# Folding a layer's normed activations over tokens ahead of the Fourier projection

## The chip, the cores and the metric

The kernel runs on one core of a Trainium2 chip. What is measured is the device time in microseconds (us) of one execution; lower is better. TensorE (PE) multiplies matrices, VectorE (DVE), ScalarE (ACT) and GpSimd (POOL) do everything else, and SyncE (SP) issues the transfers between the chip's memory and the on-chip buffer. PE writes into eight PSUM banks.

## The reference

Two layers over 1040 tokens (16 meta tokens and 1024 others) of 1024 features. In each layer the normed input goes through one projection whose columns belong to four groups (pooling, Fourier, a bidirectional state-space scan "SSD", attention); each group mixes in its own way, is gated, and one output projection adds the result to the input.

```python
for i in range(DEPTH):
    hn = rmsnorm(h, norm_w[i])
    proj = jnp.einsum("bld,de->ble", hn, w_in[i])
    (u_pool, g_pool, u_fft, g_fft, xbc, z, dt_raw, q, k, v, g_attn) = jnp.split(proj, points, axis=-1)
    y_pool = multiscale_pool(u_pool, pool_w[i], pool_scale[i]) * jax.nn.silu(g_pool)
    y_fft = fourier_mix(u_fft, fourier_w[i]) * jax.nn.silu(g_fft)
    y_ssd = ssd_mixer(xbc, z, dt_raw, ...)
    y_att = gqa_axial(q, k, v, q_norm_w[i], k_norm_w[i], cos, sin) * jax.nn.silu(g_attn)
    mixed = jnp.concatenate([y_pool, y_fft, y_ssd, y_att], axis=-1)
    h = h + jnp.einsum("ble,ed->bld", mixed, w_out[i])

def fourier_mix(u, w):
    mixed = jnp.fft.fft2(u.astype(jnp.float32), axes=(1, 2), norm="ortho").real
    return jnp.einsum("blc,cd->bld", mixed.astype(u.dtype), w)
```

The Fourier group has 512 columns, u_fft. The real part of its two-dimensional transform needs u at token n and at token 1040 - n only as their sum (for cosines) and their difference (for sines), and columns c and 512 - c likewise.

## The kernel before

Activations lie with the features on the 128 partitions and the tokens along the row: the input h is eight tiles d = 0 to 7 of 128 x 1040. Tokens go in three chunks (`CH`) of 348, 346 and 346. A 32-bit product is made of three matmuls: every operand is split into a high half, a cast on ACT (line 128), and a low half, a subtraction on DVE (line 129), and `mm3` issues high x high (line 132), high x low (133) and low x high (134) into one PSUM bank. `prenorm` writes the normed input as such halves, `s.hh` and `s.hl` (lines 186 to 188; the subtractions are shared between DVE and POOL by a table).

A projection of one 128-column tile (`proj`) is three chunks x eight d x three matmuls. Its raw weights come in two transfers of 256 KB (`wraw`, the tiles named `wr`, four buffers), and `wsplit` makes their halves `wh` and `wl` of 128 x 512 (lines 128, 129).

The Fourier projection `fft_proj` handles two column tiles i, each once as the sum of columns c and 512 - c (`kind` 0) and once as their difference (`kind` 1). The sum or difference is taken of the raw weights (line 278), so each (i, kind) is one ordinary projection of 1040 columns. Behind it DVE folds the projected u over tokens (line 283, 519 columns) and once more over half of that (`fold2`, line 289), and the result goes to memory (`md`), from where the Fourier stages read it after attention.

The order of work: each generator yields after a few instructions, `weave` runs several generators in shares, and a scheduler then fixes the order of the instructions on every engine. A layer starts with `prenorm` of the three chunks, woven with the key and value projections `kv` (`att_kv`), each chunk of keys followed by its norm and rotary work on ACT and DVE (lines 142 to 145 and 549 to 600; its last rows, line 578 before and 600 after, take the low halves of the keys, 64 x 346). The five attention stages are each woven with a share of a "fill", a long list of projections that depend on nothing but `s.hh` and `s.hl`. The string `FO` gives the fill's order: U, P, F, Z and D are projections (U is the pooling group's input, D the SSD's time steps), each C is a convolution of the SSD, R is `fft_proj`. `FN` gives the units of fill in each attention stage, `FK` the units woven with the last chunk of keys and values, and one unit is four steps. `s.h` is dropped when the prenorm is done and its eight tiles of the pool `big` (30 tiles) are used again.

The names psmm, pssc, pspv, psxx, psy are PSUM banks; smq and smn are short rotary and norm tiles.

Of the kernel before, what the change touches and what calls it, by code (L numbers as in the profile page):

```python
# [52 lines left out]
def hybrid_trunk(ctx: ExitStack, tc: tile.TileContext, io, out, depth=DEPTH):  # L53
# [22 lines left out]
    PB, KB, NPF, NACC = 2, 3, 14, 4  # L76
# [31 lines left out]
    def chunk_tile(tag, dt=F32):  # L108
        return phase["p"].tile([128, 348], dt, name=nm(tag), tag=tag, bufs=NPF if tag == "pf" else PB)
# [53 lines left out]
    def prenorm(l, s, ci):  # L163
        if ci == 0:
            s.hh = [big(F32R) for _ in range(8)]
            s.hl = [big(F32R) for _ in range(8)]
        c0, cw = CH[ci]
        ss = ps("xx")
        n = PN[l][ci]
        for i in range(n):  # L170
            eng = (nc.gpsimd, nc.vector)[i % 2]
            for d in range(i, 8, n):
                sq = sm()
                nc.scalar.activation(sq[:, :cw], s.h[d][:, c0:c0 + cw], AF.Square)
                if d == i:
                    acc = sq
                else:
                    eng.tensor_tensor(acc[:, :cw], acc[:, :cw], sq[:, :cw], op=ALU.add)
            nc.tensor.matmul(ss[:, :cw], ones, acc[:, :cw], start=(i == 0), stop=(i == n - 1))
        yield  # L180
        rs = rstd(ss[:, :cw], cw, D)
        yield
        for d in range(8):
            t = sm()
# [1 line left out]
            nc.vector.scalar_tensor_tensor(t[:, :cw], s.h[d][:, c0:c0 + cw], vec(l, V_NW + d), rs[:, :cw], op0=ALU.mult, op1=ALU.mult)
            nc.scalar.copy(hi, t[:, :cw])
            (nc.gpsimd if d in PG[ci] else nc.vector).tensor_tensor(lo, t[:, :cw], f(hi), op=ALU.subtract)  # L188
            if d % 2:
                yield  # L190
# [56 lines left out]
    def spill_dt(l, s):  # L247

        s.gd["dt"] = drp.tile([1, 40, L], F32, name=nm("gd"))
# [6 lines left out]
        for c0, cw in CH:  # L256
# [7 lines left out]
            nc.scalar.copy(t[0:40, :cw], p[64:104, :cw])  # L264
            nc.vector.tensor_tensor(t[0:40, :cw], t[0:40, :cw], p[0:40, :cw], op=ALU.add)
            nc.sync.dma_start(s.gd["dt"][0, :, c0:c0 + cw], t[:40, :cw])

    def fft_proj(l, s):

        for i in range(2):  # L270
            c = 1 - i
            for kind in range(2):
                ws = []
                for k in (0, 4):
                    a = wraw(io["w1"][l, T_FA + i, :, k:k + 4])
                    b = wraw(io["w1"][l, T_FB + i, :, k:k + 4])
                    r = (a, b)[kind]
                    nc.vector.tensor_tensor(r[:, :, c:], a[:, :, c:], b[:, :, c:], op=(ALU.add, ALU.subtract)[kind])
                    ws += wsplit([r])
                u = yield from proj_copy(s, ws)  # L280

                def fold(o, u, op):
                    nc.vector.tensor_tensor(o[:, 1:HALF], u[:, 1:HALF], u[:, HALF + 1:L][:, ::-1], op=op)

                def fold2(dst, v):

                    w = big()[0:v.shape[0], 0:HALF + 1]
                    for o, n0, n1, op in ((0, 0, 32, ALU.add), (32, 0, 4, ALU.subtract), (36, 32, 260, ALU.add), (265, 4, 260, ALU.subtract)):
                        nc.vector.tensor_tensor(w[:, o:o + n1 - n0], v[:, n0:n1], v[:, HALF + 1 - n1:HALF + 1 - n0][:, ::-1], op=op)
                    nc.scalar.copy(w[:, 264:265], v[:, HALF // 2:HALF // 2 + 1])  # L290
                    nc.sync.dma_start(dst, w)
                if i == 0 and kind == 1:

                    y = big()[0:1, 0:HALF + 1]
                    nc.vector.tensor_copy(y, u[0:1, 0:HALF + 1])
                    fold(y, u[0:1], ALU.add)
                    fold2(s.md["ny"], y)
                if kind == 1:
                    nc.vector.memset(u[:, 0:HALF + 1:HALF], 0.0)
                fold(u, u, (ALU.add, ALU.subtract)[kind])  # L300
                fold2(s.md["r"][2 * i + kind], u[:, 0:HALF + 1])
                yield

# [415 lines left out]
    def ssd_dt(l, s):  # L719
# [9 lines left out]
        for q0 in range(0, NQ, 2):  # L729
# [289 lines left out]
    for l in range(depth):  # L1019
# [184 lines left out]
```

## Time and profile before

| | before |
|---|---|
| median of 3 runs | 2110.99 us (2107.0 to 2111.65) |
| profiled execution | 2113.91 us |
| its span, first to last instruction | 2112.0 us |
| mean granted clock of TensorE | 0.981 |
| PE busy | 1991.0 us (94%), 11880 matmuls |
| DVE busy | 1397.0 us (66%) |
| ACT busy | 1012.7 us (48%) |
| POOL busy | 369.0 us (17%) |

A line "L129" is line 129 of the kernel. A row of the trace's groups gives the line, the engine, the operation, what it writes and reads with sizes, the count, the busy time, the mean of one in ns, and the idle time of the engine just before, with what ended it. A row of a timeline starts with the start in us and the duration. Matmuls overlap in such rows, so their pace is read from their starts. A window's row gives the stretch, its length and the busy time of each engine in it.

### The profile page before, as it was taken

What the parts mean: (1) busy time and instruction counts of PE and PEld (TensorE: products, weight loads), DVE (VectorE), ACT (ScalarE), POOL (GpSimd) and SP (SyncE); (2) the same over time, 40 slices, a digit from 0 to 9 for tenths busy, and PEclk for the clock granted to TensorE, in tenths of its full rate; (3) what the DMA queues carried; (4) which work ended last, traced back from release to release, by engine and by line L of the source; (5) the groups of instructions that cost most, each with busy time, mean ns of one, the idle gap of its engine ahead of it and who ended that gap; (6) DMA issues with size and microseconds to landing.
All of it is one profiled execution on the core that took longest, in us unless ns stands there. A gap on an engine that the chain in (4) does not pass through costs nothing. (4 is left out here: it accounts for less than half of the span.)

```text
span 2112.0 us, 33087 instructions
## 1 busy us (share of the span) xinstructions
PE 1991.0 (94%) x11880; PEld 1744.1 (83%) x11880; DVE 1397.0 (66%) x2693; ACT 1012.7 (48%) x2192; POOL 369.0 (17%) x365
## 2 busy tenths in 40 slices
PE   6999999999999998998789999999999999989988
PEld 4898988688899777887779988876888995878877
DVE  5675546767665555799785755476676636477985
ACT  5544344453543546356465343436535425463562
POOL 2012122032120300013120121221312203000330
PEclk9999999999999998999899999999999999989999
DMA  4321221123232567766644221122122335877766
GB/s 139 101 75 60 67 65 57 42 74 98 92 126 97 172 207 234 203 182 186 176 123 121 68 67 55 59 61 69 65 96 98 116 117 153 248 219 198 195 180 182
DMA packets 164666, 260.99 MB, mean 124 GB/s; under 512 B 20938, under 2 KB 113678, under 8 KB 164502
## 3 DMA queue, kind: packets, MB, share of 16 engines
q1 hardware_dynamic: 161846, 249.56, 38.9%
q0 software_dynamic: 2656, 9.33, 1.7%
q8 instruction: 93, 1.52, 0.3%
q14 instruction: 71, 0.58, 0.1%
HBM read 182.92 MB, written 71.67 MB: 121 GB/s over the span
## 5 line engine op out<-in xcount | busy, mean ns | idle before, releaser
L132 PE MATMUL psmm<-big,wh 128*128 128x346 f32 (+2 forms) x1920 | 643.9, 336 | 35.3 <-ACT sms L349 12.7
L133 PE MATMUL psmm<-big,wh 128*128 128x346 f32 (+2 forms) x1920 | 628.7, 327 | 8.7 <-DVE big L129 5.6
L134 PE MATMUL psmm<-big,wl 128*128 128x346 f32 (+2 forms) x1920 | 624.6, 326 | 2.6 <-DVE wl L129 2.6
L132 PEld LDWEIGHTS psmm<-big,wh 128*128 128x128 f32 x1920 | 368.5, 192 | 84.5 <-issue 31.8
L133 PEld LDWEIGHTS psmm<-big,wh 128*128 128x128 f32 x1920 | 368.4, 192 | 17.9 <-DVE big L129 7.9
L134 PEld LDWEIGHTS psmm<-big,wl 128*128 128x128 f32 x1920 | 368.5, 192 | 5.9 <-DVE wl L129 4.3
L665 POOL TENSOR_TENSOR acc<-acc,pf 116x346 f32<-116x346 f32 (+5 forms) x216 | 221.0, 1036 | 672.9 <-ACT pf L655 537.9
L128 ACT CAST wh<-wr 128x512 fp32r<-128x512 f32 (+1 forms) x236 | 145.1, 616 | 265.2 <-PE psmm L133 182.7
L129 DVE TENSOR_TENSOR wl<-wr,wh 128x512 fp32r<-128x512 f32 x232 | 162.0, 703 | 123.0 <-ACT wh L128 121.8
L132 PE MATMUL psy<-big,wh 128*128 128x346 f32 (+2 forms) x672 | 221.2, 329 | 3.2 <-ACT big L128 2.5
L133 PE MATMUL psy<-big,wh 128*128 128x346 f32 (+2 forms) x672 | 217.3, 323 | 3.1 <-DVE big L188 2.0
L134 PE MATMUL psy<-big,wl 128*128 128x346 f32 (+2 forms) x672 | 216.5, 322 | 0.0
L655 ACT ACTIVATE pf<-psy 116x346 f32<-116x346 f32 (+4 forms) x288 | 125.4, 457 | 89.4 <-PE psy L653 88.2
L675 PE MATMUL pspv<-pf,vt 116*64 116x346 f32 (+5 forms) x864 | 165.5, 465 | 0.0
L665 DVE TENSOR_TENSOR acc<-acc,pf 116x346 f32<-116x346 f32 (+5 forms) x120 | 109.3, 911 | 75.5 <-ACT pf L655 51.0
L624 DVE TENSOR_REDUCE mx<-psy 116x1 f32<-116x346 f32 (+3 forms) x272 | 132.7, 511 | 17.3 <-PE psy L623 16.9
L132 PEld LDWEIGHTS psy<-big,wh 128*128 128x128 f32 x672 | 126.6, 188 | 15.2 <-issue 7.4
L133 PEld LDWEIGHTS psy<-big,wh 128*128 128x128 f32 x672 | 126.6, 188 | 6.9 <-DVE big L188 3.1
L134 PEld LDWEIGHTS psy<-big,wl 128*128 128x128 f32 x672 | 126.7, 189 | 0.8
L350 POOL TENSOR_TENSOR sms<-sms,sms 128x346 f32<-128x346 f32 (+2 forms) x48 | 61.9, 1292 | 355.3 <-DMA bb<-csd 230.6
L675 PEld LDWEIGHTS pspv<-pf,vt 116*64 116x64 f32 (+1 forms) x864 | 59.0, 136 | 61.7 <-issue 26.0
L352 DVE TENSOR_TENSOR sms<-sms,psmm 128x346 f32<-128x346 f32 (+2 forms) x104 | 52.8, 509 | 73.5 <-PE psmm L134 37.6
(293 smaller groups left out, 3273.0 us busy)
## 6 DMA issues: line engine op xcount, KB each, us to landing
wr<-w SPq DMA_DIRECT2D x248, 256.0 KB
sms<-hd SPq DMA_DIRECT2D x112, 173.0 KB
hd<-sms SPq DMA_DIRECT2D x96, 173.0 KB
bb<-csd SPq DMA_DIRECT2D x40, 338.0 KB
md<-big SPq DMA_DIRECT2D x24, 520.0 KB
gd<-sms SPq DMA_DIRECT2D x64, 173.0 KB
big<-gd SPq DMA_DIRECT2D x16, 520.0 KB
big<-md SPq DMA_DIRECT2D x16, 520.0 KB
```

The lines of the kernel that those rows point to most:

```text
L128: nc.scalar.copy(hi, src)
L129: nc.vector.tensor_tensor(lo, src, f(hi), op=ALU.subtract)
L132: nc.tensor.matmul(out_ps, ah, bh, start=start, stop=False)
L133: nc.tensor.matmul(out_ps, ah, bl, start=False, stop=False)
L134: nc.tensor.matmul(out_ps, al, bh, start=False, stop=stop)
L350: nc.gpsimd.tensor_tensor(o, ht, t, op=ALU.add)
L352: nc.vector.tensor_tensor(o, ht, p[:, :cw], op=ALU.add)
L624: nc.vector.tensor_reduce(mx[:qn, q, e, ci:ci + 1], p[:qn, :cw], axis=AX.X, op=ALU.max)
L655: nc.scalar.activation(pf[:n, :cw], p[:n, :cw], AF.Exp, scale=0.125)
L665: eng.tensor_tensor(accs[c0, e][:n, :cw], accs[c0, e][:n, :cw], pf[:n, :cw], op=ALU.add)
L675: nc.tensor.matmul(hold["pv"][64 * e:64 * e + 64, :cw], s.vt[:n, k, v, :], pfs[e][:n, :cw], start=(k == 0), stop=(k == len(KTS) - 1))
```

## The change

- The prenorm overwrites `s.h` with the normed value instead of writing it to a temporary tile, and `s.h` is kept until the Fourier projection is done.
- `fft_proj` first folds the normed tile d over tokens (line 269 now: the sum for kind 0, the difference for kind 1; even d on DVE, odd d on POOL), splits the 522 folded columns into halves (tile `fr`, its source `fo`), and multiplies these by the weights: for each d two column tiles i x two halves of 262 and 260 columns x three matmuls, accumulated over d in four PSUM banks at once. Then ACT copies the four banks out and `fold2` (line 274 now) folds once more. The projection so has 522 columns instead of 1040.
- The weights come in groups of four d: two raw tiles for each i, with the addition or subtraction of raw weights at line 295 now. A group fills the four `wr` buffers.
- It leaves the fill (R is gone from `FO`) and is woven, 18 steps, with the last chunk of keys and values, in place of the 12 steps of U that stood there. `FN` goes from 9, 17, 17, 16, 27 units to 12, 14, 14, 15, 22, `PS`, the share given to the pooling stage's steps, from 60 to 68.
- One column (the Nyquist column of the Fourier group), which the fold over columns left in the first row of a tile, is now a 41st row of the product for the SSD's time steps, and `fft_middle` folds it, as part of D.
- The folding stage has a tile pool of its own; the exponentials' tiles of attention (`chunk_tile`) are taken from a pool that is opened when that one is closed.

```diff
-    FK, GP = 3, 24
-    FN = (9, 17, 17, 16, 27)
+    GP = 24
+    FN = (12, 14, 14, 15, 22)
...
-    FO = 'UPFDCCCCCRCCCZ'
+    FO = 'UPFDCCCCCCCCZ'
...
-            t = sm()
+            t = s.h[d][:, c0:c0 + cw]
...
-            nc.vector.scalar_tensor_tensor(t[:, :cw], s.h[d][:, c0:c0 + cw], vec(l, V_NW + d), rs[:, :cw], op0=ALU.mult, op1=ALU.mult)
+            nc.vector.scalar_tensor_tensor(t, t, vec(l, V_NW + d), rs[:, :cw], op0=ALU.mult, op1=ALU.mult)
...
+    def fold(o, u, op, eng=None):
+        (eng or nc.vector).tensor_tensor(o[:, 1:HALF], u[:, 1:HALF], u[:, HALF + 1:L][:, ::-1], op=op)
...
+    def fft_proj(l, s, pool):
+
+        half = [(0, HALF // 2 + 2), (HALF // 2 + 2, HALF // 2)]
...
+        for kind in range(2):
+            op = (ALU.add, ALU.subtract)[kind]
+            p = [[ps(x) for x in ("sc", "pv")], [ps("xx"), ps("xx")]]
+            for d in range(8):
+                if d % 4 == 0:
+                    ws = []
+                    for i in range(2):
+                        c = 1 - i
+                        a = wraw(io["w1"][l, T_FA + i, :, d:d + 4])
+                        b = wraw(io["w1"][l, T_FB + i, :, d:d + 4])
+                        r = (a, b)[kind]
+                        nc.vector.tensor_tensor(r[:, :, c:], a[:, :, c:], b[:, :, c:], op=op)
+                        ws.append(wsplit([r]))
+
+                t, o, r = s.h[d], tmp("fo", HALF + 2), tmp("fr", 2 * HALF + 4, F32R)
+                if kind == 0:
+                    nc.scalar.copy(o[:, 0:HALF + 1:HALF], t[:, 0:HALF + 1:HALF])
+                else:
+                    nc.gpsimd.memset(o[:, 0:HALF + 1:HALF], 0.0)
+                fold(o, t, op, (nc.vector, nc.gpsimd)[d % 2])
+                nc.gpsimd.memset(o[:, HALF + 1:HALF + 2], 0.0)
+                hi, lo = r[:, 0:HALF + 2], r[:, HALF + 2:]
+                split(hi, lo, o)
+                for i in range(2):
+                    for q, (c0, cw) in zip(p[i], half):
+                        mm3(q[:, :cw], *ws[i][d % 4], hi[:, c0:c0 + cw], lo[:, c0:c0 + cw], d == 0, d == 7)
                 yield
+            for i in range(2):
+                u = tmp("fu", HALF + 2)
+                for q, (c0, cw) in zip(p[i], half):
+                    nc.scalar.copy(u[:, c0:c0 + cw], q[:, :cw])
+                fold2(s.md["r"][2 * i + kind], u[:, 0:HALF + 1], tmp("fw", HALF + 1))
+            yield
...
+        with tc.tile_pool(name=nm("foldp"), bufs=1) as foldp:
+            run(weave((kv, 2 * PC + 4), (fft_proj(l, s, foldp), 18)))
         s.h = None
-        run(weave((kv, 2 * PC + 4), (islice(fill, FK * PC), FK * PC)))
+        phase["x"] = scope.enter_context(tc.tile_pool(name=nm("expp"), bufs=1))
```

How the order moves. On PE, in layer 0, behind the last chunk of keys and values, the kernel before has the U projection (psmm and psy, written from the normed halves in `big`):

```order
L134 MATMUL psmm_551<-big_133,wl_547 128x348
L132 MATMUL psmm_551<-big_134,wh_546 128x348
L133 MATMUL psmm_551<-big_142,wh_546 128x348
L134 MATMUL psmm_551<-big_134,wl_547 128x348
L132 MATMUL psmm_551<-big_135,wh_546 128x348
L133 MATMUL psmm_551<-big_143,wh_546 128x348
```

After the change the same place on PE has the first d of the folded projection, four banks side by side, with one row of the key's norm (L571) between:

```order
L132 MATMUL pssc_504<-fr_527,wh_513 128x262
L132 MATMUL pspv_505<-fr_527,wh_513 128x260
L132 MATMUL psxx_506<-fr_527,wh_522 128x262
L132 MATMUL psy_507<-fr_527,wh_522 128x260
L571 MATMUL psy_712<-smq_672,ct 128x346
L133 MATMUL pssc_504<-fr_527,wh_513 128x262
L134 MATMUL pssc_504<-fr_527,wl_514 128x262
L133 MATMUL pspv_505<-fr_527,wh_513 128x260
L134 MATMUL pspv_505<-fr_527,wl_514 128x260
```

U has moved behind the folded projection, whose matmuls each need a tile `fr` that DVE finishes.

On DVE, in layer 0 of the kernel after, from behind the prenorm's last subtraction: weight splits (L129 wl), folds (L269 fo), low halves of the keys (L600), low halves of the folded tiles (L129 fr), a weight addition of kind 0's second group and the first one of kind 1 (L295):

```order
L129 TENSOR_TENSOR wl_523<-wr_517,wh_522 128x512
L269 TENSOR_TENSOR fo_526<-big_81 128x519
L600 TENSOR_TENSOR big_205<-smq_426,big_203 64x346
L600 TENSOR_TENSOR big_206<-smq_426,big_204 64x346
L129 TENSOR_TENSOR wl_633<-wr_627,wh_632 128x512
L129 TENSOR_TENSOR fr_527<-fo_526,fr_527 128x522
L129 TENSOR_TENSOR fr_559<-fo_558,fr_559 128x522
L269 TENSOR_TENSOR fo_583<-big_83 128x519
L295 TENSOR_TENSOR wr_636<-wr_636,wr_638 128x512
L295 TENSOR_TENSOR wr_778<-wr_776,wr_778 128x4x127
L129 TENSOR_TENSOR fr_584<-fo_583,fr_584 128x522
L129 TENSOR_TENSOR wl_642<-wr_636,wh_641 128x512
```

The folds, splits and weight additions that stood in the attention stages, or had no counterpart, now stand in this one list ahead of the matmuls that need them.

On POOL, at the same place, the folds of the odd d (L269) and the memsets of single columns (L304) stand between the prenorm's subtractions (L188) and behind them:

```order
L304 MEMSET fo_558 128x1
L188 TENSOR_TENSOR big_143<-big_87,big_135 128x346
L269 TENSOR_TENSOR fo_558<-big_82 128x519
L188 TENSOR_TENSOR big_138<-big_82,big_130 128x346
L188 TENSOR_TENSOR big_140<-big_84,big_132 128x346
L188 TENSOR_TENSOR big_142<-big_86,big_134 128x346
L304 MEMSET fo_583 128x1
L304 MEMSET fo_602 128x1
L269 TENSOR_TENSOR fo_602<-big_84 128x519
```

Hardly any POOL work stood there before (the window's row of the prediction shows it).

More of the change, by code (lines that the diff above doesn't have):

```diff
@@ L75, in hybrid_trunk @@
     WB = (4, 5)
-    PB, KB, NPF, NACC = 2, 3, 14, 4
+    KB, NPF, NACC = 3, 14, 4
     SPARE = (('xx', 'xx', 'mm'), ('sc', 'sc', 'mm'), ('xx', 'mm', 'xx'), ('xx', 'sc', 'xx'))
@@ L80, in hybrid_trunk @@
     GA = (22, 23, 22, 13)
-    PS, WF = 60, 1.5
-    FK, GP = 3, 24
-    FN = (9, 17, 17, 16, 27)
+    PS, WF = 68, 1.5
+    GP = 24
+    FN = (12, 14, 14, 15, 22)
     PC = 8 // GK
     TP = 0
-    FO = 'UPFDCCCCCRCCCZ'
+    FO = 'UPFDCCCCCCCCZ'
     GF = 0
@@ L108, in chunk_tile @@
     def chunk_tile(tag, dt=F32):
-        return phase["p"].tile([128, 348], dt, name=nm(tag), tag=tag, bufs=NPF if tag == "pf" else PB)
+        return phase["x"].tile([128, 348], dt, name=nm(tag), tag=tag, bufs=NPF)
     def bb():
@@ L183, in prenorm @@
         for d in range(8):
[L184 removed]
+            t = s.h[d][:, c0:c0 + cw]
             hi, lo = s.hh[d][:, c0:c0 + cw], s.hl[d][:, c0:c0 + cw]
[L186 to L188 removed]
+            nc.vector.scalar_tensor_tensor(t, t, vec(l, V_NW + d), rs[:, :cw], op0=ALU.mult, op1=ALU.mult)
+            nc.scalar.copy(hi, t)
+            (nc.gpsimd if d in PG[ci] else nc.vector).tensor_tensor(lo, t, f(hi), op=ALU.subtract)
             if d % 2:
@@ L247, in spill_dt @@
     def spill_dt(l, s):
-        s.gd["dt"] = drp.tile([1, 40, L], F32, name=nm("gd"))
+        s.gd["dt"] = drp.tile([1, 41, L], F32, name=nm("gd"))
         w = []
@@ L263, in spill_dt @@
             t = sm("s")
[L264 to L301, printed above, removed]
-                yield
@@ new lines, in spill_dt, with fold2 @@
+            nc.scalar.copy(t[0:41, :cw], p[64:105, :cw])
+            nc.vector.tensor_tensor(t[0:41, :cw], t[0:41, :cw], p[0:41, :cw], op=ALU.add)
+            nc.sync.dma_start(s.gd["dt"][0, :, c0:c0 + cw], t[:41, :cw])
+    def fold(o, u, op, eng=None):
+        (eng or nc.vector).tensor_tensor(o[:, 1:HALF], u[:, 1:HALF], u[:, HALF + 1:L][:, ::-1], op=op)
+    def fold2(dst, v, w):
+        for o, n0, n1, op in ((0, 0, 32, ALU.add), (32, 0, 4, ALU.subtract), (36, 32, 260, ALU.add), (265, 4, 260, ALU.subtract)):
+            nc.vector.tensor_tensor(w[:, o:o + n1 - n0], v[:, n0:n1], v[:, HALF + 1 - n1:HALF + 1 - n0][:, ::-1], op=op)
+        nc.scalar.copy(w[:, 264:265], v[:, HALF // 2:HALF // 2 + 1])
+        nc.sync.dma_start(dst, w)
@@ new lines, in fft_proj, with tmp @@
+    def fft_proj(l, s, pool):
+        half = [(0, HALF // 2 + 2), (HALF // 2 + 2, HALF // 2)]
+        def tmp(tag, n, dt=F32, bufs=2):
+            return pool.tile([128, n], dt, name=nm(tag), tag=tag, bufs=bufs)
+        for kind in range(2):
[23 more added lines that the diff above has]
+                        mm3(q[:, :cw], *ws[i][d % 4], hi[:, c0:c0 + cw], lo[:, c0:c0 + cw], d == 0, d == 7)
+                yield
+            for i in range(2):
[4 more added lines that the diff above has]
+            yield
@@ L304, in silu_, with fft_middle @@
+    def fft_middle(s):
+        u = big()[0:1]
+        nc.sync.dma_start(u[:, :L], s.gd["dt"][0, 40:41])
+        fold(u, u, ALU.add)
+        fold2(s.md["ny"], u[:, 0:HALF + 1], big()[0:1, 0:HALF + 1])
+        yield
     def silu_(aps):
@@ L733, in ssd_dt @@
             x, e, u, dt, t1 = [v[:, i * w:i * w + w] for i in range(5)]
-            nc.sync.dma_start(x[R], s.gd["dt"][0, :, q0 * QC:q0 * QC + w])
+            nc.sync.dma_start(x[R], s.gd["dt"][0, R, q0 * QC:q0 * QC + w])
             nc.vector.tensor_scalar(x[R], x[R], vec(l, V_DTB)[R], None, op0=ALU.add)
@@ L1024, in hybrid_trunk @@
         conv = iter([ssd_conv(l, s, t) for t in range(8)])
-        parts = {"U": spill(l, s, T_UP, 4, "u"), "P": spill(l, s, T_GP, 4, "p", s.ch), "D": chain(spill_dt(l, s), ssd_dt(l, s)), "F": spill(l, s, T_GF, 4, "f", s.ch),
-                 "Z": spill(l, s, T_Z, 4, "z", s.ch), "R": fft_proj(l, s)}
+        parts = {"U": spill(l, s, T_UP, 4, "u"), "P": spill(l, s, T_GP, 4, "p", s.ch), "D": chain(spill_dt(l, s), ssd_dt(l, s), fft_middle(s)), "F": spill(l, s, T_GF, 4, "f", s.ch),
+                 "Z": spill(l, s, T_Z, 4, "z", s.ch)}
         fill = chain(*[parts[x] if x in parts else next(conv) for x in FO])
@@ L1170, in _layout @@
     wdt[:, :, :40] = w_in[:, :, o_dt + r40]
+    wdt[:, :, 40] = w_in[:, :, o_uf + 256]
     wdt = wdt.reshape(DEPTH, 8, 128, 64).transpose(0, 2, 1, 3)
```

## The prediction

> **What bounds the kernel now.** I read the page first, then the windows, then single timelines. The page's first two parts give the busy time of each engine and the span in 40 slices of 53 us:
>
> ```profile
> PE 1991.0 (94%) x11880; PEld 1744.1 (83%) x11880; DVE 1397.0 (66%) x2693; ACT 1012.7 (48%) x2192; POOL 369.0 (17%) x365
> PE   6999999999999998998789999999999999989988
> DVE  5675546767665555799785755476676636477985
> POOL 2012122032120300013120121221312203000330
> GB/s 139 101 75 60 67 65 57 42 74 98 92 126 97 172 207 234 203 182 186 176 123 121 68 67 55 59 61 69 65 96 98 116 117 153 248 219 198 195 180 182
> ```
>
> TensorE (PE) is at nine tenths nearly throughout. But a share near 94% doesn't say that every removed matmul is worth its time, so I looked at the stretches in which the old Fourier projection runs and at those in which the new stage will stand (columns: window, length, busy time and instructions of PE, weight loads, DVE, ACT, POOL, granted clock):
>
> ```profile
> 66.50:112.00 45.50, 44.85 (x270) 42.75 (x271) 22.33 (x46) 22.63 (x47) 0.00 (x0) 1.00 0.39 121
> 1114.00:1164.00 50.00, 50.00 (x305) 48.01 (x306) 27.56 (x60) 25.44 (x53) 0.00 (x0) 1.00 0.39 117
> 480.00:545.00 65.00, 65.00 (x388) 56.33 (x385) 49.34 (x92) 28.98 (x56) 11.72 (x12) 1.00 0.30 97
> 1580.00:1640.00 60.00, 59.98 (x359) 50.88 (x358) 35.79 (x80) 31.16 (x65) 14.47 (x12) 1.00 0.32 107
> ```
>
> The last two rows hold the old projection of either layer: PE is busy for all 65 and 60 us. The first two hold the place right behind the prenorm, when the value and key projections run out and the fill (the U projection) keeps PE full, while VectorE (DVE) works half the time and GpSimd (POOL) not at all. So there PE is the bound today, and it is fed with work that can be done anywhere.
>
> **The change, part by part.** *What is taken away.* A layer loses 4 tiles x 3 chunks x 8 k x 3 = 288 matmuls of 346 or 348 columns. Busy times of matmuls overlap, so I price them by their starts:
>
> ```profile
> 90.75 0.32 PE L133 MATMUL psmm<-big,wh 128*128 128x346 f32 x1
> 92.33 0.32 PE L134 MATMUL psmm<-big,wl 128*128 128x346 f32 x1
> 805.39 0.28 PE L132 MATMUL psy<-big,big 128*128 128x260 f32 x1
> 805.99 0.28 PE L134 MATMUL psy<-big,big 128*128 128x260 f32 x1
> ```
>
> Ten steps lie between the first two rows: 1.58 / 10 = 0.158 us for 346 columns. Five lie between the other two: 0.60 / 5 = 0.12 us for 260. Removed: 288 x 0.158 = 45.5 us a layer. Added: 2 kinds x 8 d x 2 i x 2 halves x 3 = 192 matmuls of 262 or 260 columns, 192 x 0.121 = 23.2 us. If PE were the bound in the new stage too, two layers would save 2 x 22.3 = 44.6 us. That is the ceiling, 2113.9 - 44.6 = 2069 for the profiled execution.
>
> *What sets the new stage's length.* It isn't PE. Ahead of each d's 12 matmuls (1.45 us) stand a fold over tokens, a cast to the high half (ACT) and a subtraction for the low half (DVE), and every group of four d needs two additions of raw weights and two weight splits. I price these by the nearest rows (mean ns of one in the last column before any idle time):
>
> ```profile
> L129 DVE TENSOR_TENSOR wl<-wr,wh 128x512 fp32r<-128x512 f32 x232 | 162.0, 703 | 123.0 <-ACT wh L128 121.8
> L283 DVE TENSOR_TENSOR big<-big 128x519 f32<-128x519 f32 x8 | 6.9, 869 | 0.0
> L278 DVE TENSOR_TENSOR wr<-wr,wr 128x508 f32<-128x508 f32 x8 | 5.8, 729 | 4.3 <-DMA wr<-w 4.3
> L128 ACT CAST wh<-wr 128x512 fp32r<-128x512 f32 x232 | 143.5, 620 | 260.4 <-PE psmm L133 182.7 <-PE psy L133 36.3 <-DMA wr<-w 24.1
> 1060.16 0.51 DVE L129 TENSOR_TENSOR big<-big,big 128x346 fp32r<-128x346 f32 x1
> 1060.59 0.51 DVE L178 TENSOR_TENSOR smn<-smn,smn 128x348 f32<-128x348 f32 x1
> 1062.73 0.68 DVE L129 TENSOR_TENSOR wl<-wr,wh 128x512 fp32r<-128x512 f32 x1
> ```
>
> Back to back, a 346-column operation starts 0.43 us after the one before while its row says 0.51: one takes its row less 0.08. So an undisturbed 512-column one is 0.61, and one of 519 or 522 I estimate at 0.62 by size. In layer 0 the order of DVE between the last subtraction of the prenorm and the last low half of the stage has 10 weight splits (6.1), 16 low halves (9.9), 8 folds (5.0), 5 weight additions (3.1), the rotary work of the last key chunk (eight operations at 0.43: 3.4), four 64-row low halves of keys (1.7) and eight small pieces of the second fold (1.3): 30.5 us. In layer 1 one weight addition (0.6), a second rotary chain (3.4) and two prenorm subtractions come to it: 35.1 us.
>
> *What POOL's half of the folds takes from DVE.* Eight of the 16 folds stand on POOL. They aren't free for DVE:
>
> ```profile
> 1067.49 1.19 POOL L188 TENSOR_TENSOR big<-smn,big 128x348 fp32r<-128x348 f32 x1 [10.93 <-ACT big L187]
> 1068.89 0.96 POOL L188 TENSOR_TENSOR big<-smn,big 128x348 fp32r<-128x348 f32 x1 [0.21 <-ACT big L187]
> 1068.99 1.25 DVE L188 TENSOR_TENSOR big<-smn,big 128x348 fp32r<-128x348 f32 x1
> 1070.16 0.50 DVE L352 TENSOR_TENSOR big<-sms,psmm 128x346 f32<-128x346 f32 x1
> ```
>
> A DVE subtraction of 0.51 that starts inside a POOL operation of 0.96 takes 1.25: it ends 0.39 behind POOL's end, so it is held 0.74. The next, which reads PSUM, isn't lengthened. A 519-column fold on POOL I estimate at 0.96 x 519 / 348, or 1.43, less a fixed part of 0.09: 1.34. Bounds for what it takes from DVE: nothing (DVE happens to read PSUM or to wait) and 1.34. Nearly all DVE work here has two SBUF inputs, so I take 0.9, two thirds; 8 x 0.9 = 7.2 us a layer (0 to 10.7). The Trainium skill, SBUF — State Buffer, section "Who interferes with whom", has a rule against this part: a DVE instruction with two SBUF inputs contends with a GpSimd instruction that reads SBUF, and the one that issues second blocks fully. The held row bears it out. By it alone, with DVE always second, the sum would take the upper bound, 3.5 us a layer more.
>
> *Waits.* (1) The kernel has four raw-weight buffers, and one group of four d now fills all four; the next group's 256 KB loads can start only as these are split, and DVE's first weight addition for the next kind stands right behind the split that frees its buffer, so all folds and low halves behind it on DVE wait too. The idle times "<-DMA wr<-w" in the rows of L278 (4.3 us in 8) and L128 (24.1) show that such waits exist already, small. A landing takes up to 4.6 us in the row below, and a group's 1.05 MB takes 4.2 us at 248 GB/s, the best slice of the page: 8.8 us, against some 10 us of DVE work in a group. Bounds per group: 0 to 5 us. As the loads overlap most of the group's work I take 2 us a layer.
>
> ```profile
> 2074.39 4.63 DMA sms<-hd
> ```
>
> (2) Between the kinds PE must end d = 7, ACT copies four PSUM banks and only then comes to the next kind's high halves: between nothing (two d already folded ahead) and four copies at 0.5, two casts and a 1.5 us burst, some 5; I take 3 in layer 0 and 2.5 in layer 1, where more independent DVE work stands at that place. (3) The last d's matmuls, 1.6 us, come behind the last low half; that is fixed.
>
> *Sum.* Layer 0: 30.5 + 7.2 + 2 + 3 + 1.6 = 44.3, layer 1: 35.1 + 7.2 + 1.5 + 2.5 + 1.6 = 47.9. Where the stage starts is read from the last prenorm subtractions:
>
> ```profile
> 65.81 0.93 DVE L188 TENSOR_TENSOR big<-smn,big 128x346 fp32r<-128x346 f32 x2
> 1114.32 0.51 DVE L188 TENSOR_TENSOR big<-smn,big 128x346 fp32r<-128x346 f32 x1
> 0.00:66.50 66.50, 17.46 (x49) 10.07 (x49) 0.92 0.39 124
> 66.50:112.00 45.50, 27.84 (x85) 16.00 (x85) 1.00 0.39 121
> 1081.00:1114.00 33.00, 14.46 (x45) 8.47 (x45) 1.00 0.26 74
> 1114.00:1162.00 48.00, 29.33 (x91) 17.09 (x91) 1.00 0.40 122
> ```
>
> The last four rows are line 132 alone, the first of each three matmuls. Keys and values need 48 of these in a layer. In layer 0 they are done at 66.5, and the old kernel puts 85 x 3 = 255 fill matmuls into the 45.5 us behind, or 40.3 us' worth, so 39.2 into 44.3. In layer 1 three are left at 1114, so 88 x 3 = 264, 41.7 us, lie in 48. The order of PE after puts only 9 and 5 U matmuls into the stage (1.4 and 0.8 us). So each layer owes the attention stages that fill: layer 0 gains 45.5 + 1.4 - 39.2 = 7.7, layer 1 45.5 + 0.8 - 41.7 = 4.6. Together 12.3 us.
>
> *Edits priced at nothing.* The prenorm writes in place: same operations. The Nyquist column is a row of a product that is computed anyway; its fold is four short operations on one partition, under a full PE. The old folds (L283 and the second folds) leave DVE where PE is full (the 65 us window has DVE at 49), which is worth nothing either. The attention stages get fill at 12, 14, 14, 15 in place of 9, 17, 17, 16 units. As the fill that is owed nearly equals the projection removed from there, their PE work falls by 12.3 of some 1200 us (120 to 720 us and the like stretch of layer 1); the mean shares stay as in the window of 1580, where DVE and POOL together are at 50 of 60, so PE remains their bound. If that cover failed, the 12.3 would not appear.
>
> Forecast: 2113.9 - 12.3 = 2101.6 for a profiled execution; the median of the runs shown lies 2.9 under that execution, so 2098.7, rounded to **2099**.
>
> **Rivals.** *The stage runs denser.* If POOL's folds cost DVE nothing and neither wait appears, the stages are 32 and 37 us, 12 and 11 shorter, at 0.9 us of fill a microsecond: 21 us more, 2078 on the median. For it: waits of either kind are short in the old rows. Against: the held subtraction. Half of it is likelier than all, 2085 to 2090.
>
> *The weights don't come in time.* Place: the three group changes of a layer, at the four raw buffers. Price: if a load lands only 8.8 us after its buffer comes free, and 2.5 us of addition, cast and subtraction follow ahead of the first matmul, 11.3 stand against 9 to 10 us of cover, and where the frees come late in a group, 3 to 4 us a change more than I took; 6 changes x 3.5 x 0.9 = 19 us: 2118, slower. It decides from 2.3 us a change (12.3 / 6 / 0.9). For it: all four buffers serve one group. Against: DMA moves only 121 GB/s in these windows now, and the stage has 16 loads in 44 us, 95 GB/s.
>
> *The clock.* PE works in the stage for about half the time. The old kernel shows what a wait does to it:
>
> ```profile
> 36.07 0.58 PE L132 MATMUL psmm<-big,wh 128*128 128x346 f32 x2 [2.69 <-ACT big L187]
> 813.03 0.42 PE L133 MATMUL psy<-big,big 128*128 128x260 f32 x1
> 813.89 0.42 PE L134 MATMUL psy<-big,big 128*128 128x260 f32 x1
> ```
>
> Behind that wait, and behind a longer one ahead of 812.65, matmuls of 260 columns start 0.215 apart (0.86 / 4). The whole stage so would be 192 x 0.215 = 41.3 us of PE, beside 40 of DVE: each hides the other badly where a kind ends, some 5 us a layer more, of which 9 us count: 2108, no change. Against: in the windows above the granted clock stays at 1.00 over all shorter gaps, so I hold it at one in ten. The Trainium skill, TensorE: Matmul & The Clock Gate, section "What's actually happening", puts the half rate behind an idle window of about 3.4 us; gaps of 1 to 2 us between the bursts would by that rule not bring it on. In the first row the half rate came behind 2.69 us, so here the measured row is the stricter of the two.
>
> *The attention stages don't follow.* The fill now comes later and in other shares. If a main stage falls to DVE's and POOL's pace for a twentieth of its length, the gain is gone: the same time as before, or slower together with the weights. Against it speaks the little that PE loses there (12.3 of 1200 us).
>
> **How the numbers follow.** Forecast (2092 to 2106): 0.42. Denser: 0.19. No change by the clock or by the attention stages (2107 to 2115): 0.15. Weights late, or late together with these: 0.24. A measurement of this kernel can tell about 0.2%, 4.2 us, from no change. Faster is the forecast and the denser stage, 0.61; same 0.15; slower 0.24. The range for 8 in 10 reaches from half of the denser case and a little more, 2080, to late weights at their price and a little more, 2120; the likeliest case alone is 2092 to 2106.
>
> **What would show it.** In the profile after: PE at 50 to 60% from 66 to 111 us and from 1114 to 1162, with DVE at nine tenths there; POOL folds (L269) near 1.34 us and the DVE operations inside them at twice their usual time; low halves at 0.7 us undisturbed; idle time of the weight additions (L295) "<-DMA wr<-w" at 1 to 3 us in a layer, and 3 or more a change if the weights are the bound; a granted clock of 1.00 in the stage, and 0.5 to 0.8 if the clock is; PE again at nine tenths from 120 on. I am wrong in kind if the stage is longer than 52 us in either layer, or if PE has gaps in the attention stages that it hadn't.

## The result and the profile after

| | before | after |
|---|---|---|
| median | 2111.32 us (4 runs, 2107.0 to 2114.01) | 2096.1 us (4 runs, 2093.87 to 2099.69) |
| profiled execution | 2113.91 us | 2096.46 us |
| span | 2112.0 us | 2094.6 us |

The ratio after to before is 0.9931, 95% interval 0.991 to 0.9953: faster by 15 us (10 to 19). The forecast was 2099 us, the likeliest case 2092 to 2106. The first parts of the page of after, to be held against the same rows of before:

```profile
PE 1953.7 (93%) x11688; PEld 1706.0 (81%) x11688; DVE 1437.8 (69%) x2727; ACT 1028.8 (49%) x2237; POOL 387.8 (19%) x429
PE   7799999999999998898788999999899999899988
DVE  7866556688585646698897755556876736477985
```

TensorE is busy for 37 us less and DVE for 41 us more. The span is 17.4 us shorter. The slices show where the two meet: the second slice (52 to 105 us) has DVE at eight tenths and PE at seven. In layer 1 the new stage lies in the slice from 1100 to 1152, with DVE at seven and PE at eight, and ends 10 us before that slice does.

The new stage itself, from the prenorm's last subtraction to the last folded matmul. The rows are of after's windows (length; busy PE, weight loads, DVE, ACT, POOL; clock) and of its timelines:

```profile
58.70:99.50 40.80, 31.46 (x216) 28.48 (x216) 37.92 (x62) 23.87 (x54) 13.03 (x29) 0.96 0.38 125
1099.20:1142.20 43.00, 35.62 (x240) 32.99 (x239) 39.47 (x69) 24.09 (x55) 14.16 (x29) 0.92 0.40 127
58.23 0.51 DVE L188 TENSOR_TENSOR big<-big,big 128x346 fp32r<-128x346 f32 x1
99.20 0.28 PE L134 MATMUL psy<-fr,wl 128*128 128x260 f32 x1
1098.74 0.50 DVE L188 TENSOR_TENSOR big<-big,big 128x346 fp32r<-128x346 f32 x1
1141.90 0.28 PE L134 MATMUL psy<-fr,wl 128*128 128x260 f32 x1
```

In layer 0 it is 40.8 us long, forecast 44.3; in layer 1 43.0, forecast 47.9. DVE is busy for 93 and 92% of it, PE for 77 and 83%. DVE is the bound of this stage, as forecast. But the stage starts at 58.7 us in layer 0, and the prediction put its start at 66.5, where the old prenorm ended. That start is the part that the prediction hadn't priced, and a good part of the experiments is about it.

What PE waits for in that stage (layer 0, from 46 to 100 us; sum, times, longest), then the groups of after that answer to the rows from which the stage was priced:

```profile
PE pssc L133 <- DVE fr L129: 5.1, 5, 2.1
PE pssc L132 <- ACT fr L128: 3.2, 2, 1.7
L269 POOL TENSOR_TENSOR fo<-big 128x519 f32<-128x519 f32 x16 | 26.7, 1667 | 15.5 <-DVE big L186 11.5 <-ACT fo L300 3.3
L269 DVE TENSOR_TENSOR fo<-big 128x519 f32<-128x519 f32 x16 | 13.1, 818 | 0.0
L129 DVE TENSOR_TENSOR fr<-fo,fr 128x522 fp32r<-128x522 f32 x32 | 22.4, 719 | 2.0 <-ACT fr L128 2.0
L295 DVE TENSOR_TENSOR wr<-wr,wr 128x508 f32<-128x508 f32 x8 | 7.0, 877 | 0.2 <-DMA wr<-w 0.2
L295 DVE TENSOR_TENSOR wr<-wr,wr 128x512 f32<-128x512 f32 x8 | 5.4, 679 | 0.0
```

PE waits for the low halves and for the casts. The weight additions waited 0.2 us for weights in both layers together, so the rival "the weights don't come in time" didn't happen.

### The profile page after: what moved, and what is told of

Read it like the earlier page. It is cut to its first block, busy times and chain, and to the rows that moved or that the text cites. A ratio compares the mean times of both kernels' runs of the same rounds, so it can differ in the third digit from the quotient of the medians.

```text
span 2094.6 us, 32794 instructions
## 1 busy us (share of the span) xinstructions
PE 1953.7 (93%) x11688; PEld 1706.0 (81%) x11688; DVE 1437.8 (69%) x2727; ACT 1028.8 (49%) x2237; POOL 387.8 (19%) x429
## 5 line engine op out<-in xcount | busy, mean ns | idle before, releaser
L132 PE MATMUL psmm<-big,wh 128*128 128x346 f32 (+2 forms) x1792 | 603.2, 337 | 34.2 <-ACT sms L371 15.3
L133 PE MATMUL psmm<-big,wh 128*128 128x346 f32 (+2 forms) x1792 | 588.8, 329 | 9.1 <-DVE big L129 7.6
L134 PE MATMUL psmm<-big,wl 128*128 128x346 f32 (+2 forms) x1792 | 583.8, 326 | 3.5 <-DVE wl L129 3.5
L132 PEld LDWEIGHTS psmm<-big,wh 128*128 128x128 f32 x1792 | 345.1, 193 | 77.4 <-issue 32.6
L133 PEld LDWEIGHTS psmm<-big,wh 128*128 128x128 f32 x1792 | 344.7, 192 | 21.0 <-DVE big L129 11.0
L134 PEld LDWEIGHTS psmm<-big,wl 128*128 128x128 f32 x1792 | 344.8, 193 | 7.3 <-DVE wl L129 5.3
L129 DVE TENSOR_TENSOR wl<-wr,wh 128x512 fp32r<-128x512 f32 x232 | 165.7, 719 | 107.2 <-ACT wh L128 105.0
L132 PE MATMUL psy<-big,wh 128*128 128x346 f32 (+2 forms) x608 | 199.1, 327 | 0.0
L133 PE MATMUL psy<-big,wh 128*128 128x346 f32 (+2 forms) x608 | 196.6, 323 | 1.9 <-DVE big L188 1.2
L134 PE MATMUL psy<-big,wl 128*128 128x346 f32 (+2 forms) x608 | 195.9, 322 | 0.0
L132 PEld LDWEIGHTS psy<-big,wh 128*128 128x128 f32 x608 | 114.7, 189 | 10.9 <-issue 10.0
L372 POOL TENSOR_TENSOR sms<-sms,sms 128x346 f32<-128x346 f32 (+2 forms) x48 | 57.1, 1191 | 357.8 <-DMA sms<-hd 175.8
L133 PEld LDWEIGHTS psy<-big,wh 128*128 128x128 f32 x608 | 114.8, 189 | 6.1 <-DVE big L188 1.8
L134 PEld LDWEIGHTS psy<-big,wl 128*128 128x128 f32 x608 | 114.8, 189 | 0.5
```

The lines of the kernel that those rows point to most:

```text
L129: nc.vector.tensor_tensor(lo, src, f(hi), op=ALU.subtract)
L132: nc.tensor.matmul(out_ps, ah, bh, start=start, stop=False)
L133: nc.tensor.matmul(out_ps, ah, bl, start=False, stop=False)
L134: nc.tensor.matmul(out_ps, al, bh, start=False, stop=stop)
L372: nc.gpsimd.tensor_tensor(o, ht, t, op=ALU.add)
```

## The experiments

Each kernel was run in turn with the kernel before on one chip, and is given as the ratio to it with its 95% interval. Multiplied by 2111, ratios can be compared over the table. The rows come from several chips, and medians of different rows can drift by a few us (the kernel before had medians of 2110 to 2115).

| kernel | median us | ratio to before | x 2111 |
|---|---|---|---|
| after | 2096.1 | 0.9931 (0.991 to 0.9953) | 2096 |
| after, all folds on DVE | 2089.1 | 0.9881 (0.9867 to 0.9896) | 2086 |
| after, all folds on POOL | 2101.3 | 0.9935 (0.9923 to 0.9948) | 2097 |
| after, no low halves | 2083.5 | 0.9846 (0.983 to 0.9862) | 2078 |
| before, prenorm in place | 2107.7 | 0.998 (0.9962 to 0.9998) | 2107 |
| before, eight short tiles | 2111.6 | 0.9998 (0.998 to 1.0016) | 2111 |
| before, normed value in its own ring | 2102.2 | 0.9953 (0.993 to 0.9976) | 2101 |
| after, 8 steps of U in the stage | 2083.0 | 0.9866 (0.9846 to 0.9886) | 2083 |
| after, folds on DVE, 16 steps of U | 2083.7 | 0.9865 (0.9844 to 0.9886) | 2083 |
| the same, shares 12, 13, 13, 12, 23 | 2086.9 | 0.9882 (0.9846 to 0.9918) | 2086 |
| the same, shares 12, 12, 12, 11, 26 | 2086.1 | 0.9875 (0.9841 to 0.9908) | 2085 |
| after, shares 12, 13, 13, 12, 27 | 2090.5 | 0.9895 (0.9876 to 0.9913) | 2089 |

### What a fold on POOL costs DVE

One edit, to either side:

```diff
-                fold(o, t, op, (nc.vector, nc.gpsimd)[d % 2])
+                fold(o, t, op)
```

```diff
-                fold(o, t, op, (nc.vector, nc.gpsimd)[d % 2])
+                fold(o, t, op, nc.gpsimd)
```

> All 16 folds of a layer on DVE, none on POOL. My theory (DVE's list sets the stage's length, and a fold on POOL holds one DVE operation by about 0.95 us, as the eight DVE operations of the profile after that overlap one run 0.9 to 1.1 us long): DVE gets 8 x 0.61 = 4.9 us of folds a layer and is rid of about 7.8 (layer 0) and 6.8 (layer 1) us of being held: the stages are 2 to 3 us shorter each, 4 to 6 us in all, about 2091. Rival (folds on POOL are free, DVE does other work meanwhile): 5 us a layer more, about 2106.

> All 16 folds of a layer on POOL: the disputed cost doubled. My theory: DVE is rid of 8 x 0.61 = 4.9 us a layer and is held for 8 x 0.95 = 7.6 more: 2 to 3 us a layer longer, 2100 to 2102. Rival (POOL's folds are free): 5 us a layer shorter, about 2086. A third: 16 folds of 1.3 to 1.5 us are 22 us, within the stage's 41, so POOL itself doesn't become the bound.

The two ran together: 2089.1 with no fold on POOL, 2101.3 with all of them there, 12.2 us apart (11.4 by ratios), and my theory's numbers were 2091 and 2100 to 2102. The rival had them the other way round by 20 us. The windows of layer 0's stage in these kernels (all on DVE, then all on POOL):

```profile
57.30:96.30 39.00, 31.00 (x211) 28.57 (x209) 36.25 (x71) 23.90 (x55) 1.80 (x22) 0.91 0.40 123
```

```profile
61.30:104.20 42.90, 31.99 (x205) 28.69 (x204) 39.83 (x53) 22.33 (x51) 23.09 (x36) 0.92 0.37 116
```

The stage is 39.0, 40.8 (half and half) and 42.9 us long in layer 0, and 40.4, 43.0 and 46.1 in layer 1. Moving eight folds away from DVE each time makes DVE busier, not less busy. The kernel after ran at another time, so it is compared by ratios: without folds on POOL it is 10.5 us faster, and the two stages make up 4.4 of these. The prenorm, which has folds on POOL beside it too, ends 1.4 us earlier in layer 0 as well; where the rest comes from isn't shown. With all folds on POOL the ratio can't be told from that of after (0.9935 and 0.9931), although the stages are 5.2 us longer in the traces, so that the median met the forecast of 2100 to 2102 says little. A fold on POOL that overlaps DVE looks like this in the profile of after (the first row is line 144 alone):

```profile
52.77 0.33 DVE L144 TENSOR_SCALAR smq<-smq 128x346 f32<-128x346 f32 x1
68.41 1.47 POOL L269 TENSOR_TENSOR fo<-big 128x519 f32<-128x519 f32 x1
68.03 0.69 DVE L269 TENSOR_TENSOR fo<-big 128x519 f32<-128x519 f32 x1
68.64 1.45 DVE L144 TENSOR_SCALAR smq<-smq 128x346 f32<-128x346 f32 x1
72.21 1.47 POOL L269 TENSOR_TENSOR fo<-big 128x519 f32<-128x519 f32 x1 [0.15 <-ACT fo L300]
72.44 1.62 DVE L145 TENSOR_TENSOR smq<-smq,smq 128x346 f32<-128x346 f32 x1
```

Line 144 takes 0.33 us alone and 1.45 here; line 145 0.51 and 1.62: held 1.1 each. The eight folds on POOL of layer 0 hold DVE operations for 7.8 us in sum (the excess of each over its usual time), where the prediction took 7.2. One of the eight, at 47.82 us, runs ahead of the stage, so 6.8 us fall into it. The rule of the Trainium skill that the prediction named (SBUF — State Buffer, "Who interferes with whom") goes together with the row of line 145, which has two inputs and starts behind POOL; line 144 has only one tensor input and is held all the same.

### Whether DVE sets the stage's length

The low halves' subtraction is left out and the high half multiplied in its place. The products are less exact for it, but the matmuls keep their count and size:

```diff
-                split(hi, lo, o)
+                nc.scalar.copy(hi, o)
...
-                        mm3(q[:, :cw], *ws[i][d % 4], hi[:, c0:c0 + cw], lo[:, c0:c0 + cw], d == 0, d == 7)
+                        mm3(q[:, :cw], *ws[i][d % 4], hi[:, c0:c0 + cw], hi[:, c0:c0 + cw], d == 0, d == 7)
```

> The kernel after without the low halves of the folded tiles: the subtraction on DVE is left out and the high half is multiplied in its place, so the count and size of the matmuls stay. 16 x 0.62 = 9.9 us of DVE a layer are gone. My theory (DVE sets the stage's length, PE has room): the stages are 7 to 9 us shorter each until PE (23.2 us of folded matmuls, the rest of K and V) or ACT (24 us busy) stands next: 14 to 18 us in all, about 2080. Rival (the hand-over from engine to engine or PE's half rate sets it): at most 2 us a layer, 2092 to 2096.

```profile
59.70:91.30 31.60, 27.18 (x208) 25.80 (x207) 25.81 (x45) 23.18 (x54) 11.79 (x29) 1.00 0.50 156
```

The stage of layer 0 goes from 40.8 to 31.6 us, 9.2 us for 9.9 us of DVE taken away, that of layer 1 from 43.0 to 34.3, and the time falls by 12.6 us by medians (17.9 by ratios). PE is at 86% there now, so it is near its turn. The hand-over alone doesn't set the length; DVE's list does.

### Where the earlier start comes from

In the profile of before, ACT does the squares of layer 0's last chunk only at 45.8 us, and DVE then idles for 7 us for the norm that is made from them:

```profile
45.77 3.16 ACT L174 ACTIVATE smn<-big 128x346 f32<-128x346 f32 x8
54.04 0.52 DVE L143 SCALAR_TENSOR_TENSOR smn<-psy,smn 128x346 f32<-128x346 f32 x1 [7.03 <-ACT smn L142]
```

In after the squares start at 31.4 us (its row below) and that wait isn't there.

```profile
31.39 0.87 ACT L174 ACTIVATE smn<-big 128x346 f32<-128x346 f32 x2
```

So one part of the change was put alone into the kernel before:

```diff
-            t = sm()
+            t = s.h[d][:, c0:c0 + cw]
```

> The kernel before with one part of the change alone: the prenorm writes the normed value over its input and takes no short tile for it. In the profile after, layer 0's prenorm ends at 58.7 us, in the one of before at 66.8, behind an idle DVE of 7.0 us (54.04). Theory A (the six short smn tiles held up the last chunk's squares): here too that wait goes and the prenorm ends at 58 to 60; since PE has U fill there before, the time falls by 1 to 4 us, 2107 to 2110. Theory B (the earlier end comes from what is woven with it): the wait stays, time 2111.

What theory A expects came: the squares start at 30.5 us, the wait is gone, the prenorm ends at 58.0. The window from 0 to 120 us of before, then a first square and the same window of this kernel:

```profile
0.00:120.00 120.00, 98.85 (x507) 85.17 (x508) 72.68 (x143) 65.75 (x139) 17.88 (x22) 0.96 0.37 118
```

```profile
30.53 0.48 ACT L174 ACTIVATE smn<-big 128x346 f32<-128x346 f32 x1
...
0.00:120.00 120.00, 105.96 (x569) 94.62 (x570) 82.05 (x163) 65.64 (x141) 17.32 (x22) 0.96 0.40 124
```

PE has issued 62 more matmuls by 120 us, 9.8 us at 0.158 us each, of the same kernel's work. The attention stages then run 9.7 us ahead of before to their end (their last score matmul starts at 727.2 us, in before at 736.8), and the whole span is 9.9 us shorter, so layer 1 adds next to nothing. The runs together show less than this one trace: 4 us by the ratio (0.4 to 8), 7.4 by the medians of the runs taken in turn (2115.1 and 2107.7). What makes the difference isn't on record.

How the short tiles did it took two runs. First, eight in place of six:

```diff
-    SMB = {"n": 6, "s": 4}
+    SMB = {"n": 8, "s": 4}
```

> The kernel before with eight short tiles (smn) in place of six, and the prenorm not in place. If it is these tiles that held up the squares of the last chunk in layer 0 (45.8 us in the profile of before, 30.5 to 39 with the prenorm in place), they start earlier here too, DVE's wait of 7.0 us at 54 us shrinks or goes, and the profiled execution is 5 to 10 us under the kernel before. If what counts is another thing that the in-place form changes, squares and wait stay where they are: no change.

No change, and the squares and the wait stayed:

```profile
44.52 3.17 ACT L174 ACTIVATE smn<-big 128x346 f32<-128x346 f32 x8
...
52.79 0.52 DVE L143 SCALAR_TENSOR_TENSOR smn<-psy,smn 128x346 f32<-128x346 f32 x1 [7.02 <-ACT smn L142]
```

Two more tiles don't help: theory A in that form fell. The tiles of one ring are handed out in turn, so a square of the next chunk can't have one before the eight normed values ahead of it have had theirs. So the normed value got a ring of its own, of only two tiles:

```diff
-    SMB = {"n": 6, "s": 4}
+    SMB = {"n": 6, "s": 4, "t": 2}
...
-            t = sm()
+            t = sm("t")
```

> The kernel before, with the prenorm's normed value in a ring of its own of two short tiles instead of the ring of six that the squares use too; not in place. In the run with eight tiles in one ring nothing moved (the squares of layer 0's last chunk stayed at 44.5 us), because each tile of a ring is handed out in turn: the squares stand behind the eight normed values of the chunk before, whatever the count. If that is it, the squares start earlier here, DVE's wait of 7.0 us goes and 7 to 10 us are gone by 120 us in the profile, 2103 to 2108. If it is something else in the in-place form, the squares stay at 44 to 46 us and so does the time.

The squares run from 28.7 us, the 7 us wait is gone and by 120 us PE has issued 57 more matmuls than before:

```profile
28.70 0.87 ACT L174 ACTIVATE smn<-big 128x346 f32<-128x346 f32 x2
...
0.00:120.00 120.00, 106.71 (x564) 94.94 (x565) 80.36 (x162) 65.68 (x140) 16.45 (x22) 0.96 0.40 124
```

The ratio is 0.9953, 10 us less (5 to 15). Its profiled execution was the slowest of its runs (2114.5 us), so only its first 120 us are read here. So it is the shared ring, and the in-place form helps because it takes the normed values out of it.

### Whether the stage has room for U

```diff
-            run(weave((kv, 2 * PC + 4), (fft_proj(l, s, foldp), 18)))
+            run(weave((kv, 2 * PC + 4), (fft_proj(l, s, foldp), 18), (islice(fill, 8), 8)))
...
-    FN = (12, 14, 14, 15, 22)
+    FN = (10, 14, 14, 15, 22)
```

> The kernel after with eight steps of the fill (U, 48 matmuls of 346 columns a layer, 7.6 us of PE) woven into the folded projection, and two units less in the first attention stage. My theory (DVE sets the stage's length, PE waits there some 9 us in layer 0 and 7 in layer 1): U's matmuls fall into PE's gaps, and what the stage pays is two or so more weight splits on DVE (1.2 us): 5 to 6 us gained a layer, 10 to 12 in all, about 2085. Rival (every added step delays the folded matmuls, and the raw-weight buffers are shared with it): the stage grows by what U takes, no gain, 2096.

2083.0 us, where 2085 was expected: 13 us under after. With the folds on DVE as well and 16 steps (`FN` 8, 14, 14, 15, 22):

> All folds on DVE (as in the run that had this alone, 2089), and 16 steps of U woven into the stage. If both gains add, 2089 - 10 to 14 = 2075 to 2079; if the fill only takes the time that the held operations left, 2085 to 2089.

2083.7 us: the two gains don't add. The windows of layer 0's stage, and one later, of this kernel:

```profile
56.20:103.40 47.20, 46.61 (x315) 44.32 (x316) 39.21 (x73) 27.44 (x60) 1.66 (x22) 0.95 0.43 139
...
160.00:180.00 20.00, 19.18 (x94) 15.52 (x93) 10.84 (x21) 8.98 (x22) 5.09 (x6) 0.91 0.19 63
```

PE is now at 99% in the stage. But from 160 to 180 us, where after has 128 matmuls in 20 us, there are 94: the first attention stage has run out of fill. From 161.6 to 164.5 us PE has only attention's score matmuls, 0.42 us apart, the pace of the maxima that DVE takes of them, and from 164 to 172 the granted clock is 0.79. Counted by columns, 5.4 us less of PE's work are done there than in after, and the gain is given back. I took the four units from the later stages instead:

```diff
-    FN = (8, 14, 14, 15, 22)
+    FN = (12, 13, 13, 12, 23)
```

> All folds on DVE, 16 steps of U in the stage, as in the run with both, but the four units that went into the stage are taken from the main stages and not from the first one: shares 12, 13, 13, 12, 23 in place of 8, 14, 14, 15, 22. That run lost 5.4 us from 160 to 180 us, where the first attention stage had no fill left and the clock fell to 0.91. If these come back in both layers, 2074 to 2078; if the loss only moves to a later stage, 2082 to 2086.

> As the one before with shares 12, 12, 12, 11, 26: more of the fill kept for the pooling stage. If fill is worth the same in each stage, the same time as 12, 13, 13, 12, 23; if the pooling stage is short of it, 2 to 5 us less; if the main stages fall to DVE's pace with 12 units, more.

2086.9 and 2086.1 us: no better. The window from 160 to 180 us of the first of the two:

```profile
160.00:180.00 20.00, 19.95 (x128) 19.22 (x128) 15.11 (x33) 5.44 (x11) 0.00 (x0) 1.00 0.24 80
```

The 5 us came back: counted by columns, PE is 5.1 us ahead of the run before at 180 us. At 541 us it is 5.8 us behind it, in the main stages with less fill, and at 1040 us 1.1 ahead. The loss moved, as the second half of the expectation had it. So the fill is the scarce thing: what is put into the stage is missing in another.

### Whether the pooling stage lacks fill

In after, PE is below its old share from 540 to 700 us, where the attention's last stage runs beside the pooling group. Before, after, and after with the shares 12, 13, 13, 12, 27:

```profile
120.00:540.00 420.00, 414.11 (x2447) 356.76 (x2446) 272.82 (x534) 187.87 (x409) 89.74 (x93) 1.00 0.21 67
540.00:700.00 160.00, 159.23 (x979) 147.13 (x977) 91.71 (x164) 65.84 (x133) 23.43 (x20) 1.00 0.32 109
```

```profile
120.00:540.00 420.00, 414.15 (x2465) 358.79 (x2464) 275.51 (x552) 190.20 (x421) 88.02 (x95) 1.00 0.21 63
540.00:700.00 160.00, 155.64 (x920) 136.00 (x918) 95.65 (x151) 78.27 (x145) 23.75 (x22) 1.00 0.36 121
```

```profile
120.00:540.00 420.00, 411.20 (x2417) 351.01 (x2417) 281.44 (x559) 189.40 (x424) 92.05 (x99) 0.99 0.20 61
540.00:700.00 160.00, 158.25 (x971) 144.74 (x969) 89.12 (x145) 73.00 (x139) 22.17 (x18) 1.00 0.38 128
```

```diff
-    FN = (12, 14, 14, 15, 22)
+    FN = (12, 13, 13, 12, 27)
```

> The kernel after with the fill's shares 12, 13, 13, 12, 27 in place of 12, 14, 14, 15, 22: more of it kept for the stage with the pooling group. In the profile after PE is busy for 152 of 157 us from 546 to 703 (before 168 of 169). If that stage lacks fill, 3 to 5 us a layer come back there and the earlier stages, PE-bound in both kernels, give nothing back: 2088 to 2092. If the earlier stages need their shares, what is won there is lost before: 2095 to 2100.

2090.5 us, as expected for a stage that lacks fill, though by ratios the intervals of this kernel and of after touch (0.9876 to 0.9913, 0.991 to 0.9953). In layer 0 the trace doesn't bear out that nothing is given back: PE is busier by 2.6 us from 540 to 700, and from 120 to 540 it has issued 2417 matmuls where after has 2465. At 703 us the two stand within 0.7 us of each other. The 5.0 us by which its span is shorter arise in layer 1. Whether they would come in another execution too is open.

## Why the prediction was right, point by point

- **The time**: forecast 2099, measured 2096.1; gain forecast 12.3 us on the profiled execution, 17.4 there and 15.2 by medians. It came out near, but from another sum than the one written down: a gain priced at nothing (the earlier start) is in it, and the fold gave less in layer 0 than forecast. In so far the nearness is luck. By ratios the fold with all else but the prenorm is worth about 10 us (0.9931 against 0.998; 4 to 16 if both intervals are put together), by the two spans 7.5, where the sum had 12.3.
- **The removed and added matmuls** were rightly sized. Counting each matmul by its columns at 0.158 us for 346, the work of PE falls by 45.4 us in both layers (forecast 44.6), so the ceiling was right.
- **"It isn't PE" that sets the stage**: right. DVE is at 93%, and taking 9.9 us of DVE work out makes the stage 9.2 us shorter.
- **What POOL's folds take from DVE**: 7.2 forecast, 7.8 measured in layer 0, of which 6.8 in the stage; 6.1 in layer 1's stage. The run with all folds on POOL and the one without bear out the sign, and their 11 to 12 us the size. A fold alone was put at 1.34 us on POOL; those in after that aren't held themselves last 1.29 to 1.58, and the fixed part of 0.09 in that estimate stands in no row.
- **The waits**: the weights were too dear, at 2 us in layer 0 and 1.5 in layer 1, where 0.2 were measured in both layers together. The change of kinds, 3 and 2.5 us, was too dear as well in a sum that counts DVE's time: DVE waits there for 0.57 us in layer 0 and for 0.57 and 0.84 in layer 1, as it has other work. For PE it is the longest stop. In layer 0 PE waits 1.56 and 2.06 us and then works at half rate to 85.4 us; in layer 1 one wait is 3.8 us long, in the row of PE's waits from 1090 to 1143 us, and the half rate lasts 5 us. DVE's wait in layer 0 and the row of PE:

```profile
85.59 1.15 DVE L129 TENSOR_TENSOR fr<-fo,fr 128x522 fp32r<-128x522 f32 x1 [0.57 <-ACT fr L128]
PE pssc L132 <- ACT fr L128: 4.6, 3, 3.8
```

- **The stage's length**: 44.3 and 47.9 forecast, 40.8 and 43.0 measured. In layer 0 the weights (1.8), the change of kinds (2.4) and the holding (0.4, as one fold runs ahead of the stage) are shorter than in the sum; DVE's own list and the last d's matmuls (2.1 in place of 1.6) are half a us longer each. In layer 1 the weights (1.5), the change of kinds (1.1), the holding (1.1) and DVE's list (2) are shorter: two prenorm subtractions, a fold and a weight addition that the sum has in the stage ran before its start.
- **Slips in the working**: layer 1's list adds up to 35.4 and not 35.1, and its weights stand in the sum at 1.5 where the text takes 2. The row at 1070.16 us doesn't show that an operation that reads PSUM isn't lengthened beside POOL, as POOL's operation ends at 1069.85. None of these moves the forecast by more than 1 us.
- **What was wrong**: "*Edits priced at nothing.* The prenorm writes in place: same operations." The operations are the same, but the tile that they no longer take was one of a ring in which the next chunk's squares stood in line. Alone it is worth 4 us (0.4 to 8) by ratios in the form of the change, in place, and 10 us (5 to 15) with a ring of its own; in layer 0 both are 9 to 10 us ahead by 120 us. The two intervals overlap; by them it is a quarter to two thirds of the whole gain. The wait of 7.03 us stood in the trace of before; it wasn't asked what the edit would do to it, and so the stage's start was put at 66.5 in place of 58.7.
- **The fold itself** so gained less than forecast. Counted by columns, PE has done 89.2 us of work at 120 us in before with the in-place prenorm and 73.8 in after: the stage costs 15.4 us of PE in layer 0, where the forecast's own numbers say 22.3 - 7.7 = 14.6. With 22.7 saved, 7.3 should be left. At 703 us only 2.2 are, at 730 us 1.7. Of the 5 us that went, 3.6 are PE's gaps from 540 to 703 us, in the attention's last stage; the rest isn't placed.
- **"PE remains their bound"** was therefore too simple: in the sum over the attention stages it holds (414 of 420 us from 120 to 540 in both), in the one with the pooling group it doesn't, where PE is busy for 155.6 of 160 us and was busy for 159.2. PE has gaps there that it hadn't, which is one of the two signs that the prediction gave for being wrong in kind.
- **The rivals**: the weights, refuted by 0.2 us; the clock, true for some 3 and 5 us at the change of kinds, not for the stage (0.96 and 0.92 granted); the denser stage, in part: 3.5 and 4.9 us of the 12 and 11.

## What to carry to other kernels

Where an edit takes a tile out of a ring, look at what stands behind it in that ring: a temporary that lives long holds up every later user in turn, and more tiles in the same ring need not help, while a second ring of two does. Halving the matmuls of a stage gains only what is left when the work that feeds them sets the pace: price the feeding engine's list first, and put independent matmuls into the gaps, as far as those aren't needed elsewhere. Work moved to POOL wasn't taken off DVE here, where both read the on-chip buffer: the eight folds moved there held DVE for 7.8 us, and on DVE they would have been 4.9.

## What the runs showed of the hardware

A POOL operation can be held as well. Two of the folds in after last 2.73 us in place of 1.3 to 1.6 (two more 1.86 and 2.04), at 83.45 and 1126.54 us, where DVE issues operations with two inputs back to back from just before it; the slowest in the run with all folds on POOL is 2.56 us. The rows of the first; none of the three DVE operations is lengthened:

```profile
83.14 0.68 DVE L269 TENSOR_TENSOR fo<-big 128x519 f32<-128x519 f32 x1
83.45 2.73 POOL L269 TENSOR_TENSOR fo<-big 128x519 f32<-128x519 f32 x1
83.75 1.27 DVE L295 TENSOR_TENSOR wr<-wr,wr 128x508 f32<-128x508 f32 x2
```

DVE operations with one tensor input are held too: line 144, a multiplication and addition with constants on 346 columns, took 1.45 us beside a POOL fold and 0.33 alone, in the rows shown above.

The half rate came behind two waits of 1.56 and 2.06 us with a few matmuls between them:

```profile
79.83 0.39 PE L132 MATMUL pssc<-fr,wh 128*128 128x262 f32 x1 [1.56 <-ACT fr L128]
82.66 0.58 PE L133 MATMUL pssc<-fr,wh 128*128 128x262 f32 x1 [2.06 <-DVE fr L129]
83.04 0.42 PE L134 MATMUL pssc<-fr,wl 128*128 128x262 f32 x1
85.22 0.42 PE L132 MATMUL pspv<-fr,wh 128*128 128x260 f32 x1
```

From 83.0 to 85.2 us matmuls of 260 columns start 0.22 us apart, and from 85.6 on 0.12. By the Trainium skill (TensorE: Matmul & The Clock Gate, "What's actually happening") the half rate follows an idle window of some 3.4 us. Neither wait is that long, and the two with the short burst between them are (4.4 us); whether that is the reason no run here shows.
